# A new list-scheduled instruction order for a two-block transformer kernel: another table of leads, and a replay that counts TensorE's clock in fixed periods

## The chip, the core and the metric

The kernel runs on one NeuronCore of a Trainium2 chip. Five engines work beside each other and meet at semaphores: TensorE (PE in the profile, with its weight loads apart as PEld), VectorE (DVE), ScalarE (ACT), GpSimd (POOL) and SyncE (SP), which only issues transfers here. Each runs its own instructions in the order in which they stand. The metric is the device time of one execution in microseconds (us); less is better.

## The reference

Two transformer blocks follow each other on 512 tokens of 1024 features, and the output is the second block's result.

```python
def first_block(x, mem, ...):
    h = rmsnorm(x, norm_mix)
    proj = h @ w_in                       # q, k, v, z, xbc, dt, gates
    attn = windowed_gqa_sink(q, k, v, attn_sink)
    ssd = ssd_branch(z, xbc, dt_raw, ...) # both directions, chunks of 128
    merged = (sigmoid(gate_a) * (attn @ w_attn_branch)
              + sigmoid(gate_b) * (ssd @ w_ssd_branch))
    x = x + merged @ w_out
    x = x + cross_attention(rmsnorm(x, norm_cross), rmsnorm(mem, norm_mem), ...)
    x = x + square(relu(rmsnorm(x, norm_ffn) @ w_up)) @ w_down
    return rmsnorm(x, norm_final)

def second_block(x, ...):
    h = rmsnorm_2(x, norm1_g)
    parts = split_cols(h @ w_in)
    o_a = gated_delta_rule(aq, ak, av, g, beta)   # chunks of 64, triangular solve in each
    o_b = dsa_attention(bq, bk, bv, iq, ik, iw)   # top-128 keys of an indexer
    merged = gate_a * (o_a @ w_proj_a) + gate_b * (o_b @ w_proj_b)
    x = x + merged @ w_out
    x = x + hier_moe(rmsnorm_2(x, norm2_g), ...)  # 16 experts, 2 of one group for each token
    return rmsnorm_2(x, final_norm_g)
```

## The kernel before

The 512 tokens are four blocks of 128. Each large product is made of three passes on fp32r operands: every operand is split into a high part (a cast on ScalarE) and a low part (a subtraction on VectorE or GpSimd), and TensorE adds high by high (L281), low by high (L282) and high by low (L283). So a weight goes through a raw tile from DRAM (`wr`, or `mr` for the experts' 1 MB pieces), a cast (`wh` L273, `mh` and `M` L2114) and a subtraction (`wl` L276, `ml` and `M` L2116). `M` is one pair of tiles that the experts' weights share by turns; `mh` and `ml` have buffers of their own. An activation goes through a transpose by a matmul with the identity (`tr` L364, which needs the tile `consts`), a cast (`hTh` L324) and a subtraction (`hTl` L325).

The program first emits all instructions in a plain order into a recorder. The class `Order` then replays them as a list scheduler with a model of each instruction's time, and `give` writes the order that comes out into the program: on each engine every instruction is made to follow the one before it, and tiles take their buffers in that order. At each step the replay takes, for every engine, the ready instruction with the smallest pair of (possible start plus `SLACK`, rank), and the rank is the emission position plus a number of the table `LEADS` for that engine, tile name and one of 14 stages of the program.

Places of the work that the rows and the order below speak of, by time in the execution:

- The start. SP loads `consts` (the identity), `x`, `gB` (the norm's gains, spread over the partitions), six small pieces of `vecs` and then the first weights `wr`. VectorE makes `xn` (L385), TensorE transposes it (L364).
- The change from block one to block two, about 1270 to 1300 us: for each block of tokens a step normalises twice. GpSimd forms the second half of `xn` (L1125), the small sums `ee` and `qq` (L1131 to L1134) and the factor `r` (L1135), with which VectorE and ScalarE finish `xn` for the transposes; then it multiplies the residual `x` by `gB` (L1143), which is only stored to DRAM for a later addition.
- The gated delta rule, 1355 to 1560 us: `kr`, `qr` and their transposes `kt` L1373 and `qt` L1388, `kq` L1605, and a recursion of small products `y`, `z` with `Z` and `Y` between them (L1655 to L1665).
- The sparse attention with its softmax, 1640 to 1757 us: scores `s` (L1464), transposes `pt` (L1472).
- The experts, 1900 to 2100 us: tokens are gathered into `G`, transposed into `gT`, then `gu` = gate and up products, `th` and `at`, and `y` = the down product. At the end the four blocks of tokens are gathered back, added (L2272), normalised (L1155) and stored.

```python
            w.hi, w.lo = (self.M[:, i].rearrange(...) for i in range(2))
...
        nc.scalar.copy(w.hi, raw)
        e = nc.gpsimd if self.wn % 4 < self.wpool else nc.vector
        e.tensor_tensor(w.lo, raw, w.hi.bitcast(F32), op=OP.subtract)
```

## Time and profile before

| what | value |
|---|---|
| three runs | 2119.9, 2123.61 and 2133.93 us, median 2123.61 |
| the profiled execution | 2120.89 us, of it 2119.1 us span and 1.8 us around it |
| TensorE busy | 1974.6 us (93%) |
| VectorE, ScalarE, GpSimd busy | 1326.7 us (63%), 1003.7 us (47%), 327.0 us (15%) |
| mean granted TensorE clock | 0.959 of full speed |

The profile comes from one execution, so a wait or a duration in it is compared with that execution's own 2120.89 us, which lies 2.7 us under the median of the three runs. A busy share is an average over the whole span; what a stage costs is read from that stage. "Idle before" names what ended an engine's idle time.

### The profile page before, as it was taken

The numbers are of one execution on the slowest core, as the hardware profiler recorded it, in microseconds if no ns is written. First come the engines' busy times: TensorE is split into PE (matmuls) and PEld (weight loads), VectorE is DVE, ScalarE is ACT, GpSimd is POOL, SyncE is SP. The second block draws the span as 40 slices with busy tenths as digits, with TensorE's granted clock in tenths as the row PEclk, the third lists the DMA queues.
The fourth block names the chain that finished last, engine by engine and source line by source line (L and its number), as shares of the span: only waits on it lengthen the run. The fifth ranks groups of instructions, "written<-read, shape, count | busy, mean of one in ns | idle before, by whom it ended". The sixth has DMA issues, their size and how long they took to land. (4 is left out here: it accounts for less than half of the span.)

```text
span 2119.1 us, 28828 instructions
## 1 busy us (share of the span) xinstructions
PE 1974.6 (93%) x10730; PEld 1659.6 (78%) x10730; DVE 1326.7 (63%) x2301; ACT 1003.7 (47%) x2018; POOL 327.0 (15%) x323
## 2 busy tenths in 40 slices
PE   7999999999999999999999998899899889878795
PEld 7889988888888879888888887788677767666573
DVE  4777547768888575553344347699882444358685
ACT  4555467666778743442232326222422232246573
POOL 0000000000101020021001124041110202034334
PEclk9999999999999999999999999799999689889998
DMA  5222264233433563223333333252133006838856
GB/s 159 86 76 69 91 199 139 85 115 103 126 106 113 176 230 107 67 87 97 92 90 101 98 110 120 61 145 77 48 115 120 11 16 203 309 123 313 303 175 170
DMA packets 131292, 266.49 MB, mean 126 GB/s; under 512 B 22256, under 2 KB 67696, under 8 KB 127050
## 3 DMA queue, kind: packets, MB, share of 16 engines
q1 hardware_dynamic: 127690, 256.20, 37.8%
q0 software_dynamic: 3456, 8.39, 1.6%
q8 instruction: 86, 1.41, 0.3%
q14 instruction: 60, 0.49, 0.1%
HBM read 242.86 MB, written 25.35 MB: 127 GB/s over the span
## 5 line engine op out<-in xcount | busy, mean ns | idle before, releaser
L276 DVE TENSOR_TENSOR wl<-wr,wh 128x1024 fp32r<-128x1024 f32 (+1 forms) x272 | 313.0, 1151 | 345.5 <-ACT wh L273 325.0
L273 ACT CAST wh<-wr 128x1024 fp32r<-128x1024 f32 (+1 forms) x272 | 264.6, 973 | 485.9 <-PE mm L282 227.7
L281 PE MATMUL mm<-hTh,wh 128*128 128x512 f32 (+1 forms) x1056 | 406.5, 386 | 3.7 <-ACT hTh L324 2.4
L282 PE MATMUL mm<-hTl,wh 128*128 128x512 f32 (+1 forms) x1056 | 405.1, 384 | 0.4 <-DVE hTl L325 0.2
L283 PE MATMUL mm<-hTh,wl 128*128 128x512 f32 (+1 forms) x1056 | 405.5, 385 | 0.0
L281 PEld LDWEIGHTS mm<-hTh,wh 128*128 128x128 f32 x1056 | 200.9, 191 | 38.7 <-ACT hTh L324 3.3
L282 PEld LDWEIGHTS mm<-hTl,wh 128*128 128x128 f32 x1056 | 201.1, 191 | 34.9 <-DVE hTl L325 0.9
L283 PEld LDWEIGHTS mm<-hTh,wl 128*128 128x128 f32 x1056 | 201.2, 191 | 34.5 <-DVE wl L276 0.4
L281 PE MATMUL mm<-wh,hTh 128*128 128x256 f32 x512 | 148.0, 289 | 2.4 <-DVE zg L1688 1.7
L282 PE MATMUL mm<-wl,hTh 128*128 128x256 f32 x512 | 147.6, 288 | 1.1 <-DVE wl L276 1.1
L283 PE MATMUL mm<-wh,hTl 128*128 128x256 f32 x512 | 147.8, 289 | 0.0
L716 POOL TENSOR_TENSOR xw<-xt,dtT 128x256 f32<-128x256 f32 (+1 forms) x32 | 30.5, 970 | 545.1 <-ACT xt L694 531.8
L281 PEld LDWEIGHTS mm<-wh,hTh 128*128 128x128 f32 x512 | 98.9, 193 | 3.4 <-DVE zg L1688 1.8
L282 PEld LDWEIGHTS mm<-wl,hTh 128*128 128x128 f32 x512 | 98.9, 193 | 2.2 <-DVE wl L276 1.5
L283 PEld LDWEIGHTS mm<-wh,hTl 128*128 128x128 f32 x512 | 99.0, 193 | 0.1
L654 DVE SCALAR_TENSOR_TENSOR cv<-mm,vecs,cv 128x510 f32<-128x510 f32 (+1 forms) x128 | 95.6, 747 | 2.9 <-ACT cv L647 0.4
L1093 POOL TENSOR_TENSOR ul<-r,uh 128x512 fp32r<-128x512 f32 x32 | 41.7, 1304 | 284.1 <-ACT uh L1092 268.5
L740 ACT ACTIVATE cs<-cs,ncs 128x128 f32<-128x128 f32 x256 | 79.7, 393 | 3.2 <-DMA cs<-csd 3.2
L282 PE MATMUL sa<-wl,uh 128*128 128x512 f32 x180 | 70.6, 392 | 0.1
L283 PE MATMUL sa<-wh,ul 128*128 128x512 f32 x180 | 70.1, 389 | 0.0
L281 PE MATMUL sa<-wh,uh 128*128 128x512 f32 x180 | 63.8, 396 | 0.0
L912 DVE SCALAR_TENSOR_TENSOR x<-sa,x 128x512 f32<-128x512 f32 x54 | 37.2, 690 | 31.6 <-PE sa L283 31.5
(616 smaller groups left out, 4447.7 us busy)
## 6 DMA issues: line engine op xcount, KB each, us to landing
mr<-in_w_egu_dram SPq DMA_DIRECT2D x32, 1024.0 KB, 7.4
wr<-in_win_b_dram SPq DMA_DIRECT2D x59, 512.0 KB, 3.6
cs<-csd SPq DMA_DIRECT2D x64, 256.0 KB, 4.9
wr<-in_w_up_dram SPq DMA_DIRECT2D x32, 512.0 KB, 3.7
wr<-in_w_down_dram SPq DMA_DIRECT2D x32, 512.0 KB, 3.6
wr<-in_w_ed_dram SPq DMA_DIRECT2D x32, 512.0 KB, 4.0
wr<-in_w_b_dram SPq DMA_DIRECT2D x29, 512.0 KB, 3.6
wr<-in_win_a_dram SPq DMA_DIRECT2D x18, 512.0 KB, 3.6
```

The source lines that it names most:

```text
L273: nc.scalar.copy(w.hi, raw)
L276: e.tensor_tensor(w.lo, raw, w.hi.bitcast(F32), op=OP.subtract)
L281: mm(out, lh, rh, start=start, stop=False, skip_group_check=skip)
L282: mm(out, lh, rl, start=False, stop=False, skip_group_check=skip)
L283: mm(out, ll, rh, start=False, stop=stop, skip_group_check=skip)
L654: nc.vector.scalar_tensor_tensor(ov, iv, self.cw(ct, tap), ov, op0=OP.mult, op1=OP.add)
L716: nc.gpsimd.tensor_tensor(xw[:, d0:d1], h3(xt[c])[:, None].to_broadcast([128, d1 - d0, 4, 64]), self.dtdec[:, c, d0:d1, H][:, :, :, None]. ...
L740: nc.scalar.activation(cb[d][:, h, :], cb[d][:, h, :], AF.Identity, bias=self.ncs[:, c, d, hh])
L912: nc.vector.scalar_tensor_tensor(xv, ps, scale, xv, op0=OP.mult, op1=OP.add)
L1093: nc.gpsimd.tensor_tensor(ul[:, j, :], r, uh[:, j, :].bitcast(F32), op=OP.subtract)
```

## The change

The instructions are the same ones, with as many on each engine; their order differs. Four things differ in the code. The table `LEADS` has all new numbers. ScalarE's `SLACK` goes from 300 to 500. The replay's model of TensorE's clock is another: before, a gap on TensorE of more than 1.7 us made the matmuls after it slow for a fixed time; now the replay's time is cut into fixed periods, counted from the program's start, the matmul work of each is summed, and in a period after one with too little work the matmuls run at half speed. And `runs`, which keeps matmuls on alternating halves of the array together, now also takes those that use half of the columns.

```diff
 LEADS = {
-    ('SP', 'x', 0): 44, ('SP', 'gB', 0): 145, ('DVE', 'mhalf', 0): -29, ('SP', 'wr', 0): 454, ('ACT', 'wh', 0): -31, ('DVE', 'wl', 0): 309,
...
+    ('SP', 'gB', 0): 118, ('SP', 'consts', 0): 563, ('DVE', 'mhalf', 0): -362, ('SP', 'wr', 0): 644, ('ACT', 'wh', 0): 320, ('DVE', 'wl', 0): -49,
...
-SLACK = {"PE": 100.0, "ACT": 300.0}
+SLACK = {"PE": 100.0, "ACT": 500.0}
...
-SWITCH, HOLD_V, HOLD_G = 190.0, 150.0, 100.0
+SWITCH, HOLD_V, HOLD_G, WINDOW = 190.0, 150.0, 100.0, 3413.333
...
-            if self.mode[k] == (64, 128):
+            if self.mode[k] in ((64, 128), (128, 64)):
                 o = i.outs[0].bass_ap.tensor.name
-                if cur and (self.ins[cur[-1]].tile_position[0] == i.tile_position[0] or (o not in banks and len(banks) == 2)):
+                if cur and (self.mode[cur[-1]] != self.mode[k] or tuple(self.ins[cur[-1]].tile_position) == tuple(i.tile_position)
+                            or (o not in banks and len(banks) == 2)):
                     close()
...
-        landed = slow = until_v = until_g = 0.0
+        landed = until_v = until_g = 0.0
+        work = []
...
             if e == PE:
-                if s - free[PE] > 1700.0:
-                    slow = s + (7000.0 if s - free[PE] > 3300.0 else 3700.0)
-                if s < slow:
-                    d *= 1.88
+
+                at, rest = s, d
+                while rest > 1e-9:
+                    w = int(at / WINDOW)
+                    while len(work) <= w + 1:
+                        work.append(0.0)
+                    v = 0.5 if w > 0 and work[w - 1] < 0.42 * WINDOW else 1.0
+                    x = min(rest, ((w + 1) * WINDOW - at) * v + 1e-6)
+                    work[w] += x
+                    at += x / v
+                    rest -= x
+                d = at - s
```

What the table does is seen in the order itself, at three places.

SP's queue at the very start, before. The names are the tiles and the tensors in DRAM; an `x2` is two transfers.

```order
L392 DMA consts_104<-in_consts_dram 128x640
L418 DMA x_93<-in_x_dram 128x1024 x2
L418 DMA x_94<-in_x_dram 128x1024 x2
L331 DMA gB_96<-in_norm_mix_dram 128x512
L331 DMA gB_97<-in_norm_mix_dram 128x512
L401 DMA vecs_213<-in_conv_w_dram 128x160
L402 DMA vecs_213<-in_conv_b_dram 128x32
L403 DMA vecs_213<-in_ssd_norm_dram 128x16
L331 DMA vecs_213<-in_sink_dram 128x16
L331 DMA vecs_213<-in_d_skip_dram 128x32
L406 DMA vecs_213<-in_dtba_dram 64x2
L270 DMA wr_108<-in_win_b_dram 128x1024
```

SP's queue at the same place, after the change.

```order
L401 DMA vecs_213<-in_conv_w_dram 128x160
L402 DMA vecs_213<-in_conv_b_dram 128x32
L403 DMA vecs_213<-in_ssd_norm_dram 128x16
L331 DMA vecs_213<-in_sink_dram 128x16
L331 DMA vecs_213<-in_d_skip_dram 128x32
L406 DMA vecs_213<-in_dtba_dram 64x2
L418 DMA x_93<-in_x_dram 128x1024 x2
L418 DMA x_94<-in_x_dram 128x1024 x2
L331 DMA gB_96<-in_norm_mix_dram 128x512
L331 DMA gB_97<-in_norm_mix_dram 128x512
L392 DMA consts_104<-in_consts_dram 128x640
L270 DMA wr_108<-in_win_b_dram 128x1024
```

The six small pieces moved from behind the inputs to their head, and `consts`, which held the first place, now stands behind `x` and `gB`.

GpSimd at the change from block one to block two, as a piece of the difference. `x_7918` is the residual of token blocks 1 and 2, `x_7919` that of blocks 3 and 4; `r_11546` is the factor of block 2, `qq_11598` belongs to block 3.

```order
 L1135 TENSOR_TENSOR r_11546<-qq_11544,mhalf_106 128x1
 L1140 TENSOR_TENSOR r1_11547<-ee_11545,mhalf_106 128x1
+L1143 TENSOR_TENSOR x_7918<-x_7918,gB_11456 128x512
+L1143 TENSOR_TENSOR x_7918<-x_7918,gB_11457 128x512
 L1125 TENSOR_TENSOR xn_11603<-x_7919,gB_11459 128x512
 L1131 TENSOR_SCALAR ee_11599<-ss_11597 128x1
 L1132 TENSOR_SCALAR ee_11599<-ss_11597,ee_11599 128x1
+L1143 TENSOR_TENSOR x_7918<-x_7918,gB_11456 128x512
+L1143 TENSOR_TENSOR x_7918<-x_7918,gB_11457 128x512
 L1133 TENSOR_SCALAR ee_11599<-ee_11599 128x1
 L1134 TENSOR_SCALAR qq_11598<-qq_11598,ee_11599 128x1
```

Four of the eight multiplies L1143 moved from behind the last `r` to ahead of the `r` of block 3.

ScalarE among the experts, about 1990 to 2005 us, before. `wr_17479` is a weight of a down product, which takes the shared pair `M`.

```order
L2114 CAST M_16326<-mr_17192 128x1024
L324 CAST gT_16325<-tr_17589 128x512
L2114 CAST mh_17599<-wr_17477 128x1024
L2168 ACTIVATE th_17570<-gu_17525 128x256
L2114 CAST mh_17623<-mr_17287 128x1024
L2114 CAST mh_17633<-mr_17287 128x1024
L324 CAST at_17646<-at_17643 128x256
L324 CAST gT_16324<-tr_17679 128x512
L324 CAST gT_16324<-tr_17686 128x512
L2114 CAST mh_17657<-mr_17289 128x1024
L2114 CAST M_16326<-wr_17479 128x1024
L2114 CAST mh_17696<-wr_17574 128x1024
```

ScalarE at the same place, after.

```order
L2114 CAST M_16326<-mr_17192 128x1024
L324 CAST gT_16325<-tr_17589 128x512
L2114 CAST mh_17599<-wr_17477 128x1024
L2114 CAST M_16326<-wr_17479 128x1024
L2168 ACTIVATE th_17570<-gu_17525 128x256
L2114 CAST mh_17623<-mr_17287 128x1024
L2114 CAST mh_17633<-mr_17287 128x1024
L2203 ACTIVATE Y_16322<-y_17605,wl_16815 128x512
L2114 CAST M_16326<-mr_17289 128x1024
L2114 CAST mh_17657<-mr_17289 128x1024
L324 CAST at_17646<-at_17643 128x256
L324 CAST gT_16324<-tr_17679 128x512
```

The cast of `wr_17479` into `M` moved seven places ahead, past the `th` of the expert before.

GpSimd at the same place, before, and under it after. `ml` is the low part of another weight, `G` a gather.

```order
L2116 TENSOR_TENSOR ml_17537<-mr_17190,mh_17536 128x1024
L2123 DMA G_16321<-hmd_16320,idx_16680 128x1024 x2
L2116 TENSOR_TENSOR ml_17658<-mr_17289,mh_17657 128x1024
L2116 TENSOR_TENSOR M_16326<-wr_17479,M_16326 128x1024
L2116 TENSOR_TENSOR ml_17731<-mr_17384,mh_17730 128x1024
```

```order
L2116 TENSOR_TENSOR ml_17537<-mr_17190,mh_17536 128x1024
L2123 DMA G_16321<-hmd_16320,idx_16680 128x1024
L2116 TENSOR_TENSOR M_16326<-wr_17479,M_16326 128x1024
L2116 TENSOR_TENSOR ml_17658<-mr_17289,mh_17657 128x1024
L2123 DMA G_16321<-hmd_16320,idx_16680 128x1024
```

The low part of `wr_17479` moved ahead of `ml_17658` and of one gather.

## Rows read from the trace of the kernel before

**Rows 1.** The page: engines' busy time, and TensorE's clock in 40 slices.
```profile
PE 1974.6 (93%) x10730; PEld 1659.6 (78%) x10730; DVE 1326.7 (63%) x2301; ACT 1003.7 (47%) x2018; POOL 327.0 (15%) x323
...
PEclk9999999999999999999999999799999689889998
```
**Rows 2.** Windows by stage: from:to, length, busy us of each engine, clock, DMA.
```profile
50.00:690.00 640.00, 635.42 (x3682) 552.39 (x3681) 467.24 (x814) 423.56 (x1049) 39.30 (x46) 1.00 0.36 109
...
1640.00:1757.00 117.00, 97.76 (x535) 77.79 (x535) 52.55 (x156) 33.12 (x92) 16.92 (x21) 0.73 0.09 26
...
1900.00:2065.00 165.00, 145.51 (x660) 110.05 (x659) 130.26 (x150) 113.88 (x154) 69.01 (x34) 0.97 0.75 265
```
**Rows 3.** Windows at half clock: the fourteen short ones' sum, two of them, three long.
```profile
1277.30:1284.10 6.80, 5.30 (x25) 4.79 (x24) 5.83 (x12) 5.44 (x12) 5.29 (x9) 0.50 0.27 81
...
2007.70:2014.50 6.80, 5.74 (x14) 4.40 (x15) 1.98 (x2) 2.37 (x3) 1.01 (x1) 0.50 0.71 245
...
sum 68.00, PE 54.76 PEld 47.54 DVE 35.05 ACT 21.29 POOL 14.28; mean PE 3.91 PEld 3.40 DVE 2.50 ACT 1.52 POOL 1.02
...
1355.80:1379.70 23.90, 18.39 (x62) 14.14 (x62) 16.63 (x41) 5.15 (x16) 0.52 (x1) 0.50 0.03 12
...
1669.80:1686.90 17.10, 15.70 (x66) 12.25 (x66) 8.92 (x24) 4.17 (x13) 3.30 (x4) 0.50 0.06 17
...
1881.40:1898.50 17.10, 7.43 (x37) 5.81 (x37) 13.71 (x54) 3.28 (x6) 5.16 (x8) 0.50 0.30 92
```
**Rows 4.** Timeline of SP's issues at the start: start, duration, transfer.
```profile
0.74 0.40 SPq L392 DMA_DIRECT2D consts<-in_consts_dram  x1
1.20 1.85 SPq L418 DMA_DIRECT2D x<-in_x_dram  x4
...
4.04 0.45 SPq L401 DMA_DIRECT2D vecs<-in_conv_w_dram  x1
```
**Rows 5.** Timelines of DVE and PE at the start, idle time in brackets.
```profile
10.16 1.41 DVE L385 SCALAR_TENSOR_TENSOR xn<-x,r,gB 128x512 f32<-128x512 f32 x2 [9.30 <-DMA gB<-in_norm_mix_dram]
...
10.97 1.97 PE L364 MATMUL tr<-consts,xn 128*128 128x128 f32 x8 [10.97 <-DMA vecs<-in_conv_b_dram]
```
**Rows 6.** Timeline of POOL at the change of blocks.
```profile
1280.19 0.57 POOL L1135 TENSOR_TENSOR r<-qq,mhalf 128x1 f32<-128x1 f32 x1
...
1286.01 11.18 POOL L1143 TENSOR_TENSOR x<-x,gB 128x512 f32<-128x512 f32 x8
```
**Rows 7.** Waits of PE, 1395 to 1447 us: total, times, longest.
```profile
PE kt L1373 <- DVE kr L1346: 1.6, 4, 0.6
PE kq L1605 <- DVE qk L1611: 1.5, 3, 0.6
PE qt L1388 <- DVE qr L1346: 1.4, 1, 1.4
```
**Rows 8.** Waits of PE, 1495 to 1560 us.
```profile
PE y L1665 <- DVE Z L1663: 3.3, 7, 0.9
```
**Rows 9.** The expert at 2004 us: PE's wait, then timelines of POOL and ACT.
```profile
PE y L282 <- POOL M L2116: 4.1, 1, 4.1
...
2003.07 2.36 POOL L2116 TENSOR_TENSOR ml<-mr,mh 128x1024 fp32r<-128x1024 f32 x1 [0.70 <-issue]
2005.39 3.32 POOL L2116 TENSOR_TENSOR M<-wr,M 128x1024 fp32r<-128x1024 f32 x1
...
1997.79 0.39 ACT L2168 ACTIVATE th<-gu 128x256 f32<-128x256 f32 x1 [4.29 <-PE gu L283]
...
2002.83 1.04 ACT L2114 CAST M<-wr 128x1024 fp32r<-128x1024 f32 x1
```
**Rows 10.** Waits of PE, 1640 to 1757 us.
```profile
PE pt L1472 <- ACT s L1464: 12.8, 10, 3.1
```
**Rows 11.** Timeline of DVE at the end.
```profile
2106.66 1.28 DVE L2272 TENSOR_TENSOR x<-x,sc 128x512 f32<-128x512 f32 x2
2109.52 1.28 DVE L1155 SCALAR_TENSOR_TENSOR x<-x,r,gB 128x1024 f32<-128x1024 f32 x1 [1.58 <-POOL r L338]
```

## The prediction

> **What bounds the kernel now.** I read the page first. TensorE is busy 93% of the span, and the three passes of the large products fill it; the other engines are far from full [rows 1]. [...] Then I read the windows by stage. From 50 to 690 us TensorE works 635.4 of 640 us at full clock [rows 2]. However much the new table moves things there (by my count of places, up to 30 us each way), an order can win almost nothing, and it can lose. The losses lie behind 1270 us: the attention's softmax has 97.8 busy us of 117, at a mean clock of 0.73; the experts 145.5 of 165 [rows 2].

> Last I looked up where the clock is at 0.5. In this execution that is 20 stretches, together some 173 us: fourteen of 3.4 or 6.8 us (68 us in all, 55 of them busy), five of 17 to 24 us (95.7 us, the first at 1355.8, the last at 1881.4) and the rest of the span from 2110 us on [rows 3]. As a half clock doubles a matmul's time, the short ones cost at most 34 us and the five long ones at most 48 us. Inside the long ones TensorE is often busy (15.7 of 17.1 us) and yet slow [rows 3]; before each there were waits.

> **The change part by part.** The number of instructions per engine is equal, so no work comes or goes. The new rule in `runs` touches the products of the half-width state matmuls (`wS`, and `o` from the state), whose positions in TensorE's order hardly differ, so I cost it at nothing; no other work covers that chain, and if each of its seven steps shifted by one slow matmul of 0.21 us (worked out below) it would be 1.5 us either way, which is inside the ends of the rest. The clock model and ScalarE's slack act only through the order. So the sum is made place by place.

> *Start, plus 2.5 us.* Before, `consts` is issued at 0.74 us, `x` from 1.20, then `gB`, and only then the small pieces of `vecs`, each 0.45 us or so of SP [rows 4]. The first transpose starts at 10.97, right after `xn`, which waited for `gB` until 10.16 [rows 5]. Up to then 320 KB of `consts`, 2 MB of `x` and 0.5 MB of `gB` had come, 2.9 MB in 9.4 us, so 0.31 MB per us with the first latency inside. Now six small issues stand ahead: `x` is issued at about 0.74 + 6 x 0.45 = 3.4, 2.2 us later; `consts` no longer stands before it, which gives back 1.0 us (0.32 over 0.31); then `gB` is in at about 11.4 instead of 10.2, and `consts`, without which nothing can be transposed, another 0.8 for the second half of `gB` and 1.0 for itself behind that: 13.2 to 13.7. Less 10.97 that is 2.3 to 2.7. Ends: 1.3, if `consts` comes in beside `gB`, and 4. TensorE is full behind the start [rows 2], so the delay goes straight to the end.

> *Block one to block two, plus 3 us.* Before, all eight multiplies L1143 stand behind the chain; one takes 1.4 us (11.18 over 8) [rows 6]. Four of them now stand ahead of the factor `r` of block 3: 5.6 us of GpSimd, less the 1 us that GpSimd waited there anyway. So this `r` comes at about 1284.7 instead of 1280.19, and the one of block 4 as much later. On TensorE 19 matmuls of 256 columns stand ahead of block 3's transposes; at the half clock of that place (0.21 us each by 5.30 busy us on 25 instructions [rows 3]) they last 4 us from about 1281, to 1285. `r` plus VectorE's step on `xn` (0.7 us, as at the start [rows 5]) gives 1285.4, so there is a wait of up to 1 us, and another like it at block 4; and VectorE does two other steps ahead of block 2's `xn`, for which I put 0.8 us. Sum 3; ends 1, if the matmuls cover it, and 6.

> *Gated delta rule, minus 2.5 and minus 1.5 us.* Transposes and products wait 4.5 us in all for `kr`, `qr` and `qk` [rows 7]. The new order puts 12 to 48 matmuls between them where 7 to 24 stood, so about half of that goes (ends 0 and 4). In the recursion `y` waits seven times for `Z`, 3.3 us together [rows 8]; between `z` and `y` stand now 9 to 14 matmuls instead of 7 to 11, two or three more at each step, of about 0.1 us at full clock (half of the 0.21 above): minus 1.5 (ends plus 1 and minus 3).

> *The expert at 2004 us, minus 6 us.* TensorE waits 4.1 us for the low part of a weight in the pair `M`. Its cast came only at 2002.83, and GpSimd made another low part first (2003.07, 2.36 us) and then this one, 3.32 us from 2005.39 [rows 9]. In the new order the cast stands ahead of `th`, where ScalarE idles 4.29 us until 1997.79 [rows 9], and GpSimd has nothing ahead of it; if `M` is free by 1996, the cast of 1.04 and a subtraction of 2.36 end near 1999.5, when TensorE comes to it. That takes the 4.1 us away. The stretch 2007.7 to 2014.5 at half clock [rows 3] followed this wait; if it goes with it, 3.4 us more. I take 1.9 of these, as in the other experts the new order makes some waits longer. Sum minus 6; ends minus 8 and minus 1, the last if the gather that GpSimd now does later is waited for instead.

> *The end, minus 1.5 us.* VectorE's sum for the last block (L2272) stood behind the third block's L1155, which waited for its `r` until 2109.52 [rows 11]. Now both sums of the last block stand ahead of it, but the first L1155 stands ahead of the second block's sums and waits for its `r`. Followed step by step with 1.28 us for each pair of sums and each L1155, the last one starts 1.1 us earlier, and the last gathers are issued perhaps 0.4 us earlier. Ends: minus 3 and plus 0.5.

> *The rest, plus 0.6 us, ends minus 5 and plus 5.* `gl` is formed ahead of other matmuls and `rr` a little later near 1360 (0.6 us). The long stretches of half clock stay: at 1355.8, and from 1645 to 1757, TensorE's order is nearly unchanged, and the ten waits for the softmax, 12.8 us [rows 10], keep their releaser. The other places give and take.

> Sum: 2.5 + 3 - 2.5 - 1.5 - 6 - 1.5 + 0.6 = -5.4, so 2120.9 becomes 2115.5. The profiled execution lies 2.7 us under the median; against the median of 2123.6 I predict 2118.

> **The rivals.**

> *The clock follows, 2099 us.* If the new order breaks up most of the short stretches, two thirds of their 34 us go, 23 us; with the sum without its 1.9 of clock, -3.5, that is 2120.9 - 26.5 = 2094, or 2097 on the median's scale; I say 2099, as a few new ones will come. For it: the short ones follow waits of 1 to 5 us, of which several are shortened. Against it: nine of the fourteen lie where I found no wait that gets shorter.

> *The clock's periods lie elsewhere, 2121 us.* In the trace one can see when the clock falls and rises in one execution; it cannot be seen that the next one has it at the same distance from its start. If the chip's periods stand otherwise than those of the replay, what the table wins by hitting them is lost, the 1.9 us are lost, and gains and losses at other places cancel: -3.5 and 0 to 2 of new stretches, 2118 to 2121 on the profile's scale. [...]

> *The change of blocks starves TensorE, 2129 us.* GpSimd's four multiplies run while VectorE works with them on the same tiles, and take 1.6 instead of 1.4 us each; `r` of blocks 3 and 4 comes 5.5 us later, each with a wait of 2 us, and TensorE's clock, at 0.5 from 1277.3 to 1284.1 already, stays there for 14 us more (7 lost). Then the place costs 12 instead of 3, the start 4 instead of 2.5 and the expert gives 3 instead of 6: -5.4 + 9 + 1.5 + 3 = +8, or 2129 to 2132. It decides once block 3's transposes start over 1.5 us after the matmuls before them have ended. For it: 6.8 us at half clock there now. Against it: behind 1286 there are some 80 matmuls that need no new transposes.

> **How the numbers follow.** Chances: my sum 0.48, the clock follows 0.2, the phase (nothing to measure) 0.14, starved 0.18. The ends of the terms add to about -21 and +15 around zero if all fell one way; half of that is likelier. The range reaches to the first rival and past the last: 2096 to 2141. A measurement of this kernel can tell about 1% from no change, 21 us. Faster than 2102: the first rival and a little of the sum's tail, 0.2. Slower than 2145: some of the last rival, if further stretches follow, 0.1. Within: 0.7.

> **What will show it.** The first transpose at 13.2 to 13.7 us; block 3's transposes after 1285 (plus the start's 2.5), with waits near 1 us; waits for `kr` and `qr` under 2.5 us in all; no wait of `y` for GpSimd's `M` at 2004 and no half clock behind it; the softmax's 12 us of waits and its long slow stretches unchanged. I am wrong if the number of half-clock stretches changes by more than four, or if the reordered part before 690 us, which I cost at nothing, shows waits that were not there.

## The result, and the profile after

The change made the kernel slower: 2143.77 us median of 11 runs (2133.49 to 2147.13) against 2126.25 us for the kernel before (11 runs on the same chip, 2117.05 to 2136.97). The ratio is 1.0079, 95% interval 1.0058 to 1.0100, so 12 to 21 us. I had predicted 2118 and a range up to 2141: the time lies past the range, on the slow side. By my bound of 1% it is still the middle case, to which I gave 0.7, but the interval leaves no change out, and the sum had the other sign. The profiled execution of the change, 2133.49 us with a span of 2131.7, is its fastest of the eleven; against its median it flatters the change by 10 us. The interval is 0.2% wide on either side, so the bound of 1% with which I had put the chances was far too coarse.

The page after, to be held against [rows 1]: the engines' busy time and TensorE's clock in 40 slices.

```profile
PE 1974.9 (93%) x10730; PEld 1658.6 (78%) x10730; DVE 1330.9 (62%) x2301; ACT 1006.8 (47%) x2018; POOL 324.1 (15%) x323
...
PEclk9999999999999999999999999899999689989998
```

TensorE does the same work in the same busy time (1974.9 against 1974.6 us), so what came in this pair of profiles is waiting. The mean clock is the same too (0.959), and the number of half-clock stretches (20 in either profile, 172.8 us of the span before, 176.2 after). That holds for these two executions; what the clock does over all of them is taken up with rival A below. The window of the first stage after, which answers to [rows 2] (from:to, length, busy time of PE, PEld, DVE, ACT and POOL with the number of instructions, granted clock, DMA share, GB/s):

```profile
50.00:690.00 640.00, 632.00 (x3640) 547.60 (x3639) 458.49 (x801) 416.57 (x1025) 34.68 (x40) 1.00 0.35 107
```

From 50 to 690 us TensorE now works 632.0 of 640 us where it worked 635.4, and begins 42 matmuls fewer. That is the stretch that I had costed at nothing. A window at a fixed time holds shifted work, though, so the comparison that follows goes by work: both traces are cut at the same shares of TensorE's matmuls, and the time between the cuts is taken. With the experiments below there are many profiles for each stage, in which that stage stands in the old order or in the new one. Means in us, lowest and highest, number of profiles; kernels with an edit in the stage itself are left out. The start of a stage is on the clock of the profile before; the last row runs from the start of the last matmul to the end of the span.

```
start us  old order                   new order                 new-old
   0      17.4 (16.5-17.9, 10)     20.2 (20.1-20.3, 4)    +2.8
  17     266.6 (265.2-268.8, 10)  268.0 (267.3-268.8, 4)  +1.3
 283      67.0 (66.9-67.0, 9)      71.9 (71.6-72.5, 3)    +5.0
 350     340.6 (339.9-342.2, 10)  341.4 (340.5-342.1, 4)  +0.7
 690     265.0 (260.9-268.4, 9)   269.2 (267.8-271.3, 4)  +4.2
 955     285.0 (284.9-285.3, 11)  284.7 (284.7-284.8, 3)  -0.3
1240      60.1 (60.0-61.0, 9)      63.4 (63.4-63.4, 5)    +3.3
1300      55.0 (55.0-55.2, 10)     56.2 (56.0-56.3, 4)    +1.1
1355     206.2 (203.3-211.3, 10)  205.6 (204.6-207.6, 4)  -0.6
1560      70.0 (70.0-70.0, 10)     71.0 (71.0-71.0, 4)    +1.0
1630     132.0 (129.7-139.2, 9)   128.1 (116.5-140.6, 5)  -3.8
1760     141.2 (139.9-143.8, 9)   142.3 (141.3-143.6, 5)  +1.1
1900     167.1 (165.9-169.1, 8)   167.3 (165.8-168.3, 5)  +0.2
2066      41.2 (40.0-43.2, 9)      41.3 (39.3-42.1, 5)    +0.1
2106      12.1 (11.3-12.9, 9)       9.0 (8.7-10.2, 5)     -3.2
```

The differences add to +13.0 us, +16.2 up to the last matmul and -3.2 behind it; the timed difference is 17.5 here and, in the second timing below, 10.2 (5 to 15). So the loss is in no single place: 2.8 at the start, 11.2 between 17 and 955 us, 3.3 at the change of blocks. The ranges say which rows can be told: at 0, 283, 1240 and behind the last matmul the two do not touch. At 690 they overlap (a mean of 4.2 with spreads of 7.5 and 3.5). The softmax's -3.8 at 1630 is far inside its spread of 24. The small rows depend on how the shares are counted: by the number of matmuls alone, 350 gives +1.5, 690 +3.5, 1300 +0.7, 1355 +0.9 and 1560 -0.1, and no other row moves by more than some 0.5.

**The start.** SP and TensorE after, which answer to [rows 4, 5] (start, duration, instruction, and in brackets the idle time and what ended it):

```profile
3.69 1.99 SPq L418 DMA_DIRECT2D x<-in_x_dram  x4
...
6.94 0.47 SPq L392 DMA_DIRECT2D consts<-in_consts_dram  x1
...
14.40 1.94 PE L364 MATMUL tr<-consts,xn 128*128 128x128 f32 x8 [14.40 <-DMA consts<-in_consts_dram]
```

`x` is issued at 3.69 instead of 1.20, `consts` at 6.94 instead of 0.74, and the first transpose, which waits for `consts`, starts at 14.40 instead of 10.97.

**283 to 350 us.** What the change did there stands in SP's queue. `ma<-ta` (L641) is a store of a result that VectorE forms (`ta`, L640, from `yo`, L779); `cs<-csd` (L734) are loads that ScalarE needs for the next chunk's decay. Before, SP issued a pair of these loads at 318.14, ahead of the store:

```profile
318.14 0.93 SPq L734 DMA_DIRECT2D cs<-csd  x2
325.69 0.33 SPq L641 DMA_DIRECT2D ma<-ta  x1
```

After, three of the pairs stand behind such a store; one of them on SP's timeline, then SP's waits from 318 to 345 us (total, times, longest):

```profile
331.34 0.32 SPq L641 DMA_DIRECT2D ma<-ta  x1
331.75 0.99 SPq L734 DMA_DIRECT2D cs<-csd  x2
```

```profile
SPq L641 <- DVE ta L640: 10.7, 2, 6.8
SPq L641 <- DVE yo L779: 7.7, 1, 7.7
```

Ahead of the store at 331.34 SP waits 6.8 us for VectorE, and the loads, which need nothing from VectorE, stand behind it (the 7.7 us belong to another store, at 321.19, with no such loads right behind it). The timelines of ScalarE and TensorE after, and TensorE's waits from 320 to 480 us, show where the delay arrives:

```profile
336.12 0.99 ACT L740 ACTIVATE cs<-cs,ncs 128x128 f32<-128x128 f32 x3 [0.78 <-DMA cs<-csd]
...
342.52 1.08 PE L752 MATMUL yd<-xt,cs 128*128 128x64 f32 x8 [1.51 <-DVE cs L746]
```

```profile
PE yd L752 <- DVE cs L746: 2.9, 3, 1.5
PE yo L776 <- DVE yo L779: 1.1, 1, 1.1
```

In that window the kernel before waited only this, and not for `yo`:

```profile
PE yd L752 <- DVE cs L746: 0.6, 2, 0.4
```

Right behind the waits, from 344.4 to 347.8, the clock is granted at 0.5, which it was nowhere from 50 to 768 us in the profile before. The row of that window after:

```profile
344.40:347.80 3.40, 3.40 (x9) 2.67 (x8) 1.92 (x2) 1.16 (x2) 0.00 (x0) 0.50 0.38 124
```

At half clock the matmuls of 512 columns start 0.43 us apart (344.45 to 345.31 us), right behind it 0.23 apart (347.83 to 352.82), so the 3.4 us lose up to 1.6 us of work. In this profile these and some 3.4 us of waiting more account for the 5.0. The half clock is no necessary part of it: in the splice with the new order of block one (below) the stage takes 71.6 us with no stretch at half clock in it, and there the same waits are 4.2 and 1.0 us.

**690 to 955 us.** Two waits for `wl`, the low part of a weight, that the trace before does not have:

```profile
779.73 0.50 PE L283 MATMUL mm<-yh,wl 128*128 128x512 f32 x1 [2.67 <-DVE wl L276]
...
798.88 0.50 PE L282 MATMUL sa<-wl,mh 128*128 128x512 f32 x1 [2.42 <-DVE wl L276]
```

**The change of blocks.** GpSimd's timeline after, which answers to [rows 6], and TensorE's waits from 1280 to 1315 us:

```profile
1288.11 3.63 POOL L1143 TENSOR_TENSOR x<-x,gB 128x512 f32<-128x512 f32 x2
...
1294.34 2.51 POOL L1143 TENSOR_TENSOR x<-x,gB 128x512 f32<-128x512 f32 x2
...
1297.62 0.57 POOL L1135 TENSOR_TENSOR r<-qq,mhalf 128x1 f32<-128x1 f32 x1
```

```profile
PE tr L364 <- DVE xn L1136: 5.9, 2, 5.4
...
PE mm L282 <- DVE hTl L325: 1.5, 2, 1.3
PE mm L281 <- ACT hTh L324: 0.8, 1, 0.8
```

Four multiplies stand ahead of the `r` of block 3, which comes at 1297.62. By then the whole kernel runs 12.7 us late, so `r` itself is 4.7 us later (1297.62 - 1280.19 - 12.7). Little of that reaches TensorE. The transposes of blocks 2 and 3 after, and under them those of block 2 before:

```profile
1290.75 1.94 PE L364 MATMUL tr<-consts,xn 128*128 128x128 f32 x8 [5.45 <-DVE xn L1136]
...
1299.12 1.53 PE L364 MATMUL tr<-consts,xn 128*128 128x128 f32 x8 [0.49 <-DVE xn L1136]
```

```profile
1277.08 0.92 PE L364 MATMUL tr<-consts,xn 128*128 128x128 f32 x4 [4.44 <-DVE hTl L325]
```

Block 3's transposes wait 0.49 us (0.78 in the second profile of the change). The long wait is block 2's, and it stood there before with 4.44. Block 2's `r` is out at 1287.6, but VectorE makes two `wl` and two `hTl` before it takes that block's `xn` at 1289.49; before, it made one `wl` and took `xn` at 1275.01, 1.8 us earlier at equal work. All waits in this place are 8.2 us, and were 6.4. The half-clock stretch of this place is 10.2 us long instead of 6.8 [rows 3].

**Gated delta rule.** TensorE's waits from 1355 to 1447 us after; [rows 7] are the ones of before that I wanted to see go:

```profile
PE rsT L1558 <- DVE ny L352: 4.0, 1, 4.0
PE kq L1605 <- DVE qk L1611: 3.2, 2, 2.0
PE rsB L1572 <- DVE rr L325: 2.0, 1, 2.0
PE mm L282 <- DVE wl L276: 1.9, 1, 1.9
...
PE kt L1373 <- DVE kr L1346: 0.6, 1, 0.6
```

`kt` fell from 1.6 to 0.6 and `qt` from 1.4 to nothing, as forecast. But `kq` rose from 1.5 to 3.2, and before the window held 3.1 for `rsT`, 1.4 for `rsB` and 1.1 for `wl`: these grew by 0.9, 0.6 and 0.8. That is 2.4 won and 4.0 lost.

**The experts.** TensorE's waits from 1960 to 2066 us after, against the 4.1 us of [rows 9]:

```profile
PE y L282 <- POOL M L2116: 3.5, 2, 1.9
PE y L281 <- ACT M L2114: 3.1, 2, 1.7
PE y L282 <- DVE M L2116: 1.9, 2, 1.6
...
PE gu L281 <- ACT M L2114: 0.9, 1, 0.9
PE gu L282 <- DVE M L2116: 0.8, 1, 0.8
```

The one long wait is gone. In its place are eight short ones on the same pair `M`, 10.2 us together, where the five sums before add to 8.5 (4.1, 2.6, 0.8, 0.7 and 0.3).

### The profile page after: what moved, and what is told of

The parts are those of the page before. It is cut to its first block, busy times and chain, and to the rows that moved or that the text cites. A ratio compares the mean times of both kernels' runs of the same rounds, so it can differ in the third digit from the quotient of the medians.

```text
span 2131.7 us, 28812 instructions
## 1 busy us (share of the span) xinstructions
PE 1974.9 (93%) x10730; PEld 1658.6 (78%) x10730; DVE 1330.9 (62%) x2301; ACT 1006.8 (47%) x2018; POOL 324.1 (15%) x323
## 5 line engine op out<-in xcount | busy, mean ns | idle before, releaser
L2114 ACT CAST mh<-mr 128x1024 fp32r<-128x1024 f32 x47 | 48.7, 1049 | 18.2 <-PE y L283 9.7
```

## The experiments

My theory after the result: the loss is real waiting that the new order brings into stretches where TensorE had been full, above all before 955 us. Rival A: the clock, by chance or by its phase, made the difference, and no place holds it. Rival B: the change of blocks alone starves TensorE, as my third rival had it. Rival C: the new table and the new replay do not go together, and one of them is to blame.

Most kernels here are splices. Such a kernel computes both orders, before's (`old`: old table, slack, clock model and runs) and the change's (`new`), and takes the sequence from one of them up to the n-th matmul, then from the other. Its core, added to the changed kernel:

```diff
+def splice(order, parts):
...
+    lines = {"old": old.replay(), "new": order.replay()}
...
+    out, seen = [], set()
+    for which, upto in parts:
+        count = 0
+        for k in lines[which]:
+            if upto is not None and count >= upto:
+                break
+            count += order.type[k] == "InstMatmult"
+            if k not in seen:
+                seen.add(k)
+                out.append(k)
+    return out
...
+    order.out = splice(order, PARTS)
```

In the splices' rows a line number can stand one or more higher than in the two kernels. All ratios are to the kernel before, run on the same chip beside them (medians 2126.23 to 2128.46 us).

**One part at a time.** The new order up to matmul 290 (the start):

```diff
+PARTS = [('new', 290), ('old', None)]
```

> The changed order up to the 290th matmul (about 54 us), then the old order. Theory A (the loss is made of waits at places that moved, and they add): the profile of the change is 3.0 us late behind the start, so plus 3 us over the kernel before (2 to 4), with the first transpose near 13.5 us. Theory B (the waits are a wash, and the loss is TensorE's half-clock stretches falling elsewhere): less than 2 us either way beyond those 2.5, and no order between the parts.

Measured 2131.41 us, 1.0026 (1.0007 to 1.0045).

The new order of block one behind its start, up to some 955 us:

```diff
+PARTS = [('old', 290), ('new', 4960), ('old', None)]
```

> The old order, but from the 290th to the 4960th matmul (54 to 956 us) the changed one. Theory A: the profile of the change loses 9 to 10 us more in this stretch (some 7 to 690 us, 3 behind it), from waits of yd for cs and of yo, and one half-clock stretch near 344 us; so plus 8 to 11 us over the kernel before, the largest part. Theory B: under plus 4, with a clock share like that of before.

Measured 2139.87 us, 1.0065 (1.0040 to 1.0090): most of the whole loss, from a part that I had costed at nothing.

The change of blocks and the gated delta rule:

```diff
+PARTS = [('old', 6290), ('new', 8120), ('old', None)]
```

> The old order, but from the 6290th to the 8120th matmul (1261 to 1634 us: change of blocks, gated delta rule, indexer) the changed one. Theory A: plus 5 to 6 us (4 at the change of blocks, 1.6 in the delta rule, as the profile of the change lost there). Theory B: anywhere within 4 us of the kernel before, decided by the granted clock.

Measured 2130.64 us, 1.0025 (1.0005 to 1.0045): a small loss, where my sum had forecast a gain of about 1.

The experts and the end:

```diff
+PARTS = [('old', 8960), ('new', None)]
```

> The old order up to the 8960th matmul (1869 us), then the changed one: routing, experts and end. Theory A: plus 4 to 5 us, as the 4.3 us won at the expert of 2004 us are given back at the next experts and at the end. Theory B: within 4 us of the kernel before.

Measured 2125.19 us, 0.9999 (0.9980 to 1.0019): of the 7.5 us that my sum gained at the expert and the end, nothing that can be told from zero. The interval reaches from 4 us won to 4 us lost; the 3.2 us that this order wins behind the last matmul lie within it.

The softmax stage:

```diff
+PARTS = [('old', 8120), ('new', 8960), ('old', None)]
```

> The old order, but from the 8120th to the 8960th matmul (1634 to 1869 us: softmax, its neighbours and the loads behind it) the changed one. Theory A: the 8 us that the profile of the change won here belong to the order, so minus 6 to 8 us. Theory B: they belong to where the half-clock stretches fell in that one execution: within 3 us of the kernel before.

Measured 2125.55 us, 0.9982 (0.9954 to 1.0010). Its profile is the fastest of the splices in this stage and yet the gain cannot be told from none. The five ratios less one add to 0.97%, against 0.79% for the change; their intervals cover that. (The stretch from 956 to 1261 us is in none of the five; there the two orders take the same time within 0.3 us.)

The waits in this stage do fall, though. TensorE's waits for the softmax, 12.8 us before [rows 10], are 6.9 to 8.5 us in the five profiles with the new order, and all its waits in the stage fall from 20.7 to 21.9 us (nine old ones) to 16.5 to 18.7. That some 4 us of waiting less shorten the whole time is not shown.

Rival A falls as the main cause: the loss sits in places and comes with them. The executions on record say how much is left to the clock. Over 107 of the kernel before, run beside the experiments, and 23 of the change, the mean times differ by 14.1 us and the mean granted clocks are 0.957 and 0.955. In both kernels an execution with a lower clock takes longer; a line fitted to both, with one slope (16 us for 0.01 of clock), puts the change 10.7 us (9.7 to 11.6) above the kernel before at equal clock, and leaves some 3.4 us to the lower clock. Rival B falls as well: block one behind its start costs 0.65% without the change of blocks.

**The changed kernel a second time**, unedited:

> The changed kernel once more, to see another profile: the one on hand is the fastest of its eleven runs (2133.5 against a median of 2143.8). Theory A: the same waits as in the first profile, and a time within 3 us of that profile plus its waits. Theory B: the same order, but the half-clock stretches stand at other distances from the start, there are about 20 us more of them, and the time is near 2143.

Measured 2141.36 us, 1.0048 (1.0024 to 1.0071): slower again, a little less so.

**Table and replay apart.** The old kernel with the new table alone, then the changed kernel with the old table:

```diff
 LEADS = {
-    ('SP', 'x', 0): 44, ('SP', 'gB', 0): 145, ('DVE', 'mhalf', 0): -29,
...
+    ('SP', 'gB', 0): 118, ('SP', 'consts', 0): 563, ('DVE', 'mhalf', 0): -362,
...
```

> The old replay (old clock model, slack and runs) with the new table. The order comes out otherwise than in either kernel. If the table was fitted to its own replay, this is slower than both, by plus 15 to 40 us over the kernel before; if the replay matters little and the table makes the loss, about plus 17, as the changed kernel.

Measured 2163.16 us, 1.0138 (1.0104 to 1.0171).

> The new replay (new clock model, slack 500, runs) with the old table. If the table was fitted to its own replay, plus 10 to 40 us over the kernel before; if the replay's new clock model by itself does not hurt, within 5 us of the kernel before.

Measured 2165.89 us, 1.0158 (1.0123 to 1.0192; the diff is that of the table, reversed). Either half alone is about twice as bad as the whole, as a table fitted to its own replay would be. Rival C falls in so far as neither half is to blame by itself; what in either order costs the 29 to 34 us is not shown.

**The loads behind the store.** In the changed kernel, wherever SP's order reads `ma`, `cs`, `cs`, the store goes behind the two loads (three places):

```diff
+            if e == SP:
+                for j in range(len(line) - 2):
+                    if tuple(self.name[k] for k in line[j:j + 3]) == ("ma", "cs", "cs"):
+                        line[j:j + 3] = [line[j + 1], line[j + 2], line[j]]
```

> The changed kernel with three places of SP's queue near 310 to 340 us as before: the pair of cs loads stands ahead of the ma store instead of behind it; nothing else differs. Theory A1 (a store that waits for VectorE holds the cs loads behind it, and TensorE then waits for cs): in the profile the waits of yd for cs and of yo between 320 and 480 us fall from 4.0 and more to under 1.5 us, the half-clock stretch near 345 us is gone, and the time falls by 4 to 7 us against the changed kernel, so plus 8 to 13 over the kernel before. Rival (the waits come from ScalarE's and VectorE's order): within 2 us of the changed kernel, about plus 15, with the same waits.

The reverse in the kernel before: `cs`, `cs`, `ma` becomes `ma`, `cs`, `cs`, again at three places and with nothing else changed:

```diff
...
+                    if tuple(self.name[k] for k in line[j:j + 3]) == ("cs", "cs", "ma"):
+                        line[j:j + 3] = [line[j + 2], line[j], line[j + 1]]
```

> The kernel before with the same three places turned round: the ma store stands ahead of the cs loads. Theory A1: waits of yd for cs appear near 330 us (2 to 4 us) and the time rises by 3 to 6 us over the kernel before. Rival (order of the other engines): no change beyond 2 us.

With the loads first, the stage from 283 us takes 67.0 us instead of 71.9, exactly its time in the old order, and the half-clock stretch near 345 us is gone. With the loads last it takes 82.7 in the kernel that had 67.0, and that kernel's time rises to 2145.35 us, 1.0073 (1.0050 to 1.0096): 15.5 us timed against 15.7 in the stage. TensorE's waits from 320 to 480 us, first with the loads first, then with the loads last:

```profile
PE yd L752 <- DVE cs L746: 2.0, 2, 1.3
```

```profile
PE yd L752 <- DVE cs L746: 8.7, 3, 4.7
PE yo L776 <- DVE yo L779: 2.9, 1, 2.9
```

With the loads first the wait for `cs` falls only to 2.0 us, where I had expected under 1.5. So three swaps in SP's queue, no more, can cost as much as the whole change did. The way back, however, shows in the stage alone: the change with the loads first was timed at 2141.89 us, 1.0067 (1.0044 to 1.0090), between the change's own 1.0079 and 1.0048. A gain of 5 us lies within these intervals, and so does none.

**Narrower pieces.** The change of blocks alone, then the place of the two `wl` waits:

```diff
+PARTS = [('old', 6290), ('new', 6490), ('old', None)]
```

> The old order, but from the 6290th to the 6490th matmul (1261 to 1302 us, the change of blocks) the changed one. If the prediction's term there is right (four multiplies of GpSimd ahead of the factor r), plus 3 to 4 us over the kernel before, with block 3's transposes about 4 us later; if the loss between 1261 and 1634 us lies in the delta rule, under plus 1.

Measured 2129.05 us, 1.0012 (0.9989 to 1.0035). The stage took 63.4 us like the change's, against 60.1, with the same waits (6.0 us for `xn`, 5.5 of them at block 2's transposes). In the whole time 3 us cannot be told from none here. The piece holds GpSimd's multiplies and VectorE's order together; they were not tried apart.

```diff
+PARTS = [('old', 3600), ('new', 4100), ('old', None)]
```

> The old order, but from the 3600th to the 4100th matmul (705 to 813 us, the second branch's product with its weights and the merge) the changed one. In the profiles with the changed order TensorE waits 2.7 and 2.4 us for the low parts wl of two weights near 780 and 799 us. If these come from the order of this stretch, the stretch from 690 to 955 us takes 4 us more than before and the time rises by 3 to 5 us; if they come from what lies ahead of it, neither is seen and the time is within 2 us of the kernel before.

Measured 2127.86 us, 1.0009 (0.9983 to 1.0034). TensorE's waits from 690 to 970 us with this piece alone:

```profile
PE mm L284 <- DVE wl L277: 4.1, 3, 2.7
...
PE sa L283 <- DVE wl L277: 2.4, 1, 2.4
```

Both waits come with it, 2.7 and 2.4 us as in the change, and its stage took 268.2 us, which lies in the new order's range and still in the old one's (up to 268.4). So it is shown that this piece brings the waits, and not that they cost time, in the stage or in the whole: both spreads are wider than the 3 or 4 us in question.

The one expert:

```diff
+PARTS = [('old', 9460), ('new', 9530), ('old', None)]
```

> The old order, but from the 9460th to the 9530th matmul (1990 to 2017 us) the changed one, which casts the down product's weight into M ahead of th. The prediction's term says: the wait of 4.1 us goes and nothing comes in its place, minus 4 to 6 us. The rival, after the profiles of the change: the one pair M is given on sooner to this weight, and the wait comes back at the next users of M, so the stretch from 1900 to 2066 us is as long as before within 1 us, and so is the time.

Measured 2128.49 us, 1.0002 (0.9987 to 1.0018). TensorE's waits from 1960 to 2066 us:

```profile
PE gu L282 <- ACT M L2115: 2.6, 3, 1.3
...
PE y L283 <- POOL M L2117: 1.8, 1, 1.8
PE y L283 <- DVE M L2117: 1.8, 2, 1.5
PE gu L283 <- DVE M L2117: 1.2, 2, 0.8
...
PE y L282 <- ACT M L2115: 0.8, 1, 0.8
```

Of the 4.1 us for GpSimd's `M`, 1.8 are left, but the next users of the pair wait for it in their turn: 8.2 us together, 8.5 before. The stage got no shorter (169.8 us, where the old order takes 165.9 to 169.1).

**What is best of both**: the old order up to the softmax, then the new one.

```diff
+PARTS = [('old', 8120), ('new', None)]
```

> The old order up to the 8120th matmul (1634 us), then the changed one, so the softmax, the routing, the experts and the end in one. Its two halves alone measured 0.9982 and 0.9999 of the kernel before. If parts add, minus 3 to 6 us, the best version so far; if those were chance, within 3 us.

Measured 2124.61 us, 0.9978 (0.9948 to 1.0007), the lowest median of all, and not clear of the kernel before.

## Why the prediction was wrong

**The step that failed** is the sentence on 50 to 690 us, that an order "can win almost nothing, and it can lose", and the zero that I then put into the sum. I had counted places moved by up to 30 us there, and had looked up only the places where TensorE already waited. A stretch without waits has nothing to win, so every move in it is a risk, and the sum has to look for the instruction that now stands behind a waiting one. It measured +7.0 us (1.3, 5.0 and 0.7), and the same kind of place from 690 to 955 us, which "the rest" covered with ends of 5, +4.2. The piece with all of it timed +13.8 us (8.5 to 19). For the 5.0 the mechanism is shown in both directions: loads behind a store that waits for VectorE (the stage falls from 71.9 to 67.0 us with the loads first, and rises from 67.0 to 82.7 with the loads last). For the 4.2 the waits and the piece of order that brings them are shown, not their price; for the 1.3 and the 0.7 no cause is shown. The last line of my prediction named this case, waits before 690 us that were not there, as what would prove it wrong.

My sum was -5.4 and the stages give +13.0. Of these 18.4 us, 7.0 are that zero, 6.2 the expert, 3.4 the gated delta rule and some 3 the rest; the start and the change of blocks came within 0.3 of their terms, and the end gave 1.6 more than forecast.

**Start, plus 2.5.** Right: +2.8 in the stage, timed 1.5 to 9.6 us. The first transpose came at 14.40, 0.7 later than my bound for it, and released by `consts`, as worked out.

**Block one to block two, plus 3.** The size was right, +3.3, and that was in good part luck. The factor `r` of block 3 came 4.7 us later as worked out, but its transposes waited 0.5 to 0.8 us for it and block 4's 0.2 at most, where I had up to 1 for each. More came at block 2, to which I had given 0.8 for VectorE's steps ahead of its `xn`: that `xn` starts 1.8 us later, and TensorE's transposes of it 1.0 later. Behind block 4's transposes TensorE waits 1.1 us for `hTh` and `hTl`, which it did not before. The half-clock stretch is 3.4 us longer, which I had not counted at all.

**Gated delta rule, minus 2.5 and minus 1.5.** Of the three waits that I named two went, 2.4 us of `kt` and `qt`. The third, `kq`, and three of the same window that I had not counted grew by 4.0 us; behind the window four waits for `qr`, 2.6 us before, became 3.3. In the recursion the waits of `y` for `Z` fell from 3.3 to 1.7 us, just the 1.5 that I had forecast, but the waits of `wt` for `W` next to them rose from 0.3 to 1.7. What failed in both is that I took waits away and put none in their place. The stage gave -0.6 (+0.9 with the shares counted by number) with a spread of 8 us.

**The expert, minus 6.** The wait of 4.1 us went and its successors took it: +0.2 in the stage, nothing timed. The step that failed is the closing "if `M` is free": one pair of buffers serves every such weight, so an earlier cast takes it earlier from the one and gives it no earlier to the next. With this pair the sum of waits on `M` does not fall (8.5 us before, 8.2 with the one expert's piece, 10.2 after the whole change).

**The end, minus 1.5.** Right in sign, and more came than I had: +0.1 up to the last matmul and -3.2 behind it, -3.1 in all, just past my end of -3. The chain came in part as planned: the first L1155, now ahead of the second block's sums, waits 2.17 us for its `r`, but the last one waits 0.93 where it waited 2.13, and from the first sum to the last L1155 it takes 13.3 us (13.0 in the second profile) instead of 13.9. More of the gain lies ahead of it: the first sum starts 1.2 to 2.0 us earlier at equal work, where I had 0.4 for the gathers. VectorE's timeline after, and under it the last L1155 before:

```profile
2113.00 1.29 DVE L2272 TENSOR_TENSOR x<-x,sc 128x512 f32<-128x512 f32 x2 [7.73 <-DMA x<-yd,rows]
2116.45 1.28 DVE L1155 SCALAR_TENSOR_TENSOR x<-x,r,gB 128x1024 f32<-128x1024 f32 x1 [2.17 <-POOL r L338]
...
2126.26 1.28 DVE L1155 SCALAR_TENSOR_TENSOR x<-x,r,gB 128x1024 f32<-128x1024 f32 x1 [0.93 <-POOL r L338]
```

```profile
2113.53 1.29 DVE L1155 SCALAR_TENSOR_TENSOR x<-x,r,gB 128x1024 f32<-128x1024 f32 x1 [2.13 <-POOL r L338]
```

**The rest.** Its places add to some +3 (4.2 from 690 us on, and -3.8 in the softmax), inside the ends of 5. That the softmax's 12 us of waits would stay was wrong: they fell to about 7.

**The rivals.** "The clock follows" did not come: the changed order has as many half-clock stretches as the old one in the first pair of profiles, and over all executions a slightly lower clock (0.955 against 0.957). Three things that I had said of the stretches are put too simply. A half clock does not quite double a matmul's time: 0.43 us apart for 0.23 at 512 columns (above), and at the change of blocks before 0.21 for 0.12 at 256, so the 68 us of the short ones cost at most some 32 us. The short ones began behind or within waits of 0.9 to 7.4 us, not 1 to 5. And before the long one at 1355.8 there was no wait: TensorE was busy in all of the 20.8 us ahead of it. "The change of blocks starves TensorE" had the right sign for the wrong reason; its place cost 3.3 us, not 12, the four multiplies took 6.1 us, so 1.5 each, and the clock stayed at 0.5 there for 3.4 us more, not 14. "The clock's periods lie elsewhere" was right in what it says of the stretches, though by its own terms its time adds to 2117 to 2119 us on the profile's scale, not 2118 to 2121. The two profiles of the changed kernel, identical in every instruction, differ in the softmax: the same matmuls, nearly the same waits for `s` (7.4 and 7.3 us), and 123.0 against 128.9 us. The windows of the first and of the second profile:

```profile
1648.60:1771.60 123.00, 105.49 (x592) 82.77 (x591) 57.34 (x162) 35.10 (x94) 18.49 (x23) 0.78 0.12 37
```

```profile
1653.10:1782.00 128.90, 111.95 (x594) 87.46 (x593) 57.36 (x162) 35.09 (x94) 18.45 (x23) 0.74 0.11 36
```

## What to carry to other kernels

When an order is made anew, go first to the stretches where the bounding engine has no waits, and look in each queue that it depends on for what now stands behind a waiting instruction: a load behind a store that waits for another engine is the first thing to look for (three pairs of loads moved behind such a store cost 15.5 us here). Making one use of a shared buffer earlier need not win the wait on it (8.5 us on `M` before, 8.2 with the earlier cast); count all waits on that buffer, in both orders. An instruction that comes later can cost far less than its delay (`r` came 4.7 us later, and block 3's transposes waited 0.49 us for it): follow it to the bounding engine, and look at what already waited there. Compare up to the end of the execution: what changes behind the last matmul (3.2 us here) shows in no stage that is cut by matmuls. And where a kernel's time scatters by half a per cent from one execution to the next, compare stages at equal work over several profiles, since the difference of two profiles is not the difference of two kernels; with the granted clock of each execution on record, compare at equal clock as well.

## What the runs showed of the hardware

The scatter of TensorE's clock is larger than I had thought. The softmax stage with its 592 or 593 matmuls and busy times on the other engines that agree within 4% took from 116.5 to 140.6 us over all profiles. The granted clock falls as that time grows: the profiles at hand have 116.5 us at 0.85, 123.0 at 0.78, 128.9 at 0.74 and 140.6 at 0.65 in the new order, and 130.0 at 0.75 and 139.2 at 0.68 in the old one. The windows of this stage in the splice with the new softmax order (0.85) and in the change with the loads first (0.65), whose order is the same there:

```profile
1636.60:1753.10 116.50, 97.31 (x593) 75.97 (x592) 57.68 (x163) 35.44 (x95) 18.46 (x23) 0.85 0.12 37
```

```profile
1647.90:1788.50 140.60, 123.28 (x593) 98.03 (x592) 57.27 (x162) 35.19 (x94) 18.45 (x23) 0.65 0.10 32
```

Busy TensorE differs by 26 us on the same matmuls, and the span by 24. Whole executions follow the clock too: the 107 of the kernel before run from 2117.3 us at a mean clock of 0.961 to 2143.3 at 0.948. In the second profile of the change the clock stayed at 0.5 for one stretch of 54.6 us, in which TensorE was busy 50.6, where the first profile has 20.5 and 17.1 us with full clock between:

```profile
1669.10:1723.70 54.60, 50.58 (x220) 41.26 (x221) 21.53 (x65) 11.61 (x38) 9.34 (x13) 0.50 0.04 11
```

What decides in one execution whether such a stretch breaks off is open; with equal order and nearly equal waits it fell either way.
